# Experts of 256 slots: one matmul of 512 columns for both parts of the tokens, and down products with the weights streaming

## Chip, cores and metric

One core of one Trainium2 chip. The metric is device microseconds of one execution; smaller is better. TensorE is written PE, VectorE DVE, ScalarE ACT, GpSimd POOL, SyncE SP.

## The reference, cut to what matters

Two layers of a token-mixing block followed by a channel-mixing block; 1024 tokens of 1024 float32 numbers each. The channel mixing of the second layer is what the change touches: a router gives every token two of eight experts, and an expert is a gated two-layer network with 2816 inner features.

```python
logits = jnp.dot(xt, w_router).astype(jnp.float32)
top_logits, top_idx = lax.top_k(logits, TOP_K)
top_w = jax.nn.softmax(top_logits, axis=-1)
...
h = jax.nn.silu(lax.ragged_dot(xs, w_gate, group_sizes)) * lax.ragged_dot(xs, w_up, group_sizes)
ys = lax.ragged_dot(h, w_down, group_sizes) * top_w.reshape(-1)[order][:, None]
out = jax.ops.segment_sum(ys, tok, num_segments=n_tok)
...
x = _layernorm(DEEPNORM_ALPHA * x + (1.0 + g2) * ff, ln2_g[layer], ln2_b[layer])
```

## The kernel before, in words

**Precision.** Products of float32 are made from two parts of each operand: `split` (L350) rounds a tile to the format fp32r on ACT (the high part) and takes the rest on DVE (the low part); `wsplit` (L361) does it for weights. `mm3` (L354) then accumulates three matmuls in PSUM: high x high, high x low and low x high. In `mm3(out, a, b)` the first operand of each matmul is the one that is loaded into PE (stationary), and the second streams through it, one column after the other.

**Experts.** The eight experts are sorted by their number of tokens, and expert r (r = 0 to 7) has a fixed number of slots, `CAPS[r]` = 328, 280, 272, 264, 260, 256, 256, 256 (L36); what goes beyond is left to `overflow`. `moe` (L1342) runs the experts in a row:

- `gather` (L1094) fetches the tokens' rows from memory with indirect DMAs of POOL. `expert_in` (L1116) transposes them on PE (tile `xt`, L1125), scales them on ACT and splits them: tiles `xs`, features in partitions, slots in columns, high and low parts in tiles of their own.
- `expert_up` (L1147): for each of 22 blocks of 128 inner features, the gate and the up weights (1024 x 128 each, tiles `ew`) are split, and for each of the two and each of 8 slices k of the 1024 inputs `mm3` runs with the weights stationary and the slots streaming (tiles `eg` and `eu`, N columns each). ACT takes the Silu of `eg` from PSUM (L1166), DVE multiplies it by `eu` from PSUM (L1167), and the result is split into the tiles `eh`. Weights arrive by two DMAs of 1 MB from SP's queue for each two blocks (L1140).
- `expert_down` (L1172): for each quarter `dp` of the 1024 outputs, two blocks j of 128 outputs are accumulated over the 22 inner blocks, again with the weights stationary (tiles `dw`) and the N slots streaming (tile `ed`, outputs in partitions). ACT scales by the gate column `gcol` (L1194), PE transposes the result back to one row per slot (tile `yp`, L1200), and ACT copies it to `yr` (L1202), which a DMA of POOL writes to `ys`. For the last expert, `last_expert` (L1306) adds it to the tokens' rows instead (L1332), normalizes them (`finish`, L1278) and writes them to the output.

While expert 7's up products run, hooks (L1368) combine the results of the other experts for all 1024 tokens, in eight tiles: `combine` (L1285) gathers two result rows per token by indirect DMA, adds them on DVE (L1299), normalizes on DVE and ACT and applies two rows of the layer norm on POOL (`gain`, L782). While expert 1's run, hooks prepare the residual.

`gate_row` (L324) makes a row of the conditioning gate, one plus the gate, the same in all partitions: per 128 columns DVE makes a diagonal matrix and PE multiplies it by ones in float32.

**Order and buffers.** The order of each engine's instructions is set when the program is built, by a scheduler that simulates a timeline (L1465); engines work through their instructions in that order and wait on semaphores. PSUM has six banks for products (`bank`, L115) and two for transposes (`tbank`, L121). Six tiles `ws` hold three pairs of high and low weight parts (L75), four tiles hold raw weights (L91), three `tmp` tiles hold intermediate results (L76), and 32 tiles of 4 KB per partition (`s4`, L88) hold the rest.

Of the kernel before, what the change touches and what calls it, by code (L numbers as in the profile page):

```python
# [6 lines left out]
F32 = mybir.dt.float32  # L7
F32R = mybir.dt.float32r
I32 = mybir.dt.int32
U32 = mybir.dt.uint32  # L10
AF = mybir.ActivationFunctionType
# [22 lines left out]


CAPS = (328, 280, 272, 264, 260, 256, 256, 256)  # L36
PITCH = 1280
OVB = sum(CAPS[:-1])
FAR = 1 << 16
# [27 lines left out]
class Trunk:  # L67
# [1048 lines left out]
    def expert_in(self, r, rows, AB):  # L1116
        nc = self.nc
        N = CAPS[r]
        A, B = AB
        xs = [[self.s4([P, 3, N], F32R, f"xs{r}{x}{i}") for i in range(3)] for x in "hl"]  # L1120
        for k in range(KT):
            ps = self.tbank(f"xt{r}{k}")
            for c, t in enumerate(rows):
                n = min(P, N - c * P)
                nc.tensor.transpose(ps[:, c * P:c * P + n], t[:n, k * P:(k + 1) * P], self.ident[:n, :n])  # L1125
            u = self.tmp([P, N], f"xu{r}{k}")
            nc.scalar.activation(u, ps[:, :N], AF.Identity, bias=B[:, k:k + 1], scale=A[:, k:k + 1])  # L1127
            self.split(xs[0][k // 3][:, k % 3], xs[1][k // 3][:, k % 3], u)
        return xs

    def expert_w(self, r, f, n, queue=None):

# [14 lines left out]
    def expert_up(self, r, xs, ahead, hook):  # L1147

        nc = self.nc
        N = CAPS[r]  # L1150
        hs = [[self.s4([P, 3, N], F32R, f"eh{r}{x}{i}") for i in range(8)] for x in "hl"]
        for fb in range(0, NF, 2):
            if ahead and fb < 4:
                ws = lambda j: ahead[fb // 2 + 1](j) if fb else ahead[j](0)
            else:
                ws = self.expert_w(r, fb, 2)
            for f in (fb, fb + 1):
                pss = []
                for i, (hi, lo) in enumerate(ws(f - fb)):
                    ps = self.bank(f"e{'gu'[i]}{r}{f}")  # L1160
                    for k in range(KT):
                        self.mm3(ps[:, :N], (hi[:, k], lo[:, k]), [xs[x][k // 3][:, k % 3] for x in range(2)],
                                 k == 0, k == KT - 1)
                    pss.append(ps)
                sg = self.tmp([P, N], f"es{r}{f}")
                nc.scalar.activation(sg, pss[0][:, :N], AF.Silu)  # L1166
                nc.vector.tensor_tensor(sg, sg, pss[1][:, :N], op=OP.mult)  # L1167
                self.split(hs[0][f // 3][:, f % 3], hs[1][f // 3][:, f % 3], sg)
            hook(fb // 2)
        return hs  # L1170

    def expert_down(self, r, hs, gcol, ys, last=None):  # L1172
        nc, w = self.nc, self.w
        N, e = CAPS[r], self.ereg[r]
        nch = (N + P - 1) // P
        wv = w["moe_w_down"][0][bass.ds(e, 1)].rearrange("e (f p) n -> p (e f) n", p=P)
        if last is None:
            yr = [self.s4([P, D], F32, f"yr{r}{c}") for c in range(nch)]
        for dp in range(4):
            pss = [self.bank(f"ed{r}{dp}{j}") for j in range(2)]  # L1180
            for f0 in range(0, NF, 8):
# [14 lines left out]
            for c in range(nch):  # L1196
                n = min(P, N - c * P)
                ps = self.tbank(f"yp{r}{dp}{c}")
                for j in range(2):
                    nc.tensor.transpose(ps[:n, j * P:(j + 1) * P], yt[j][:, c * P:c * P + n], self.ident)  # L1200
                if last is None:
                    nc.scalar.activation(yr[c][:n, dp * 256:(dp + 1) * 256], ps[:n, :256], AF.Copy)  # L1202
                else:
                    last(c, dp, ps)
        if last is not None:
            return
        for c in range(nch):
            n = min(P, N - c * P)
            nc.gpsimd.dma_start(ys[BASE[r] + c * P:BASE[r] + c * P + n, :], yr[c][:n])  # L1209
# [96 lines left out]
    def last_expert(self, acc, rows, out):  # L1306
# [19 lines left out]

        done = []

        def f(c, dp, ps):
            n = min(P, N - c * P)  # L1330
            x, sl = xs[c], slice(dp * 256, (dp + 1) * 256)
            nc.vector.scalar_tensor_tensor(x[:n, sl], ps[:n, :256], ws[c][:n], x[:n, sl], op0=OP.mult, op1=OP.add)  # L1332
            if dp == 3:
                self.finish(x[:n], [a[:n] for a in rows], f"l{c}")
                s = nc.gpsimd.indirect_dma_start(out=out, out_offset=at(c, n, raw), in_=x[:n], in_offset=None,
                                                 bounds_check=S - 1, oob_is_err=False)
                for o in done:
                    self.tc.declare_no_dep(s.ins, o.ins, reason="each slot belongs to one token")
                done.append(s)
        return f  # L1340

    def moe(self, l, xn, AB, pieces, back, out):  # L1342
# [16 lines left out]
        hook = none = lambda i: None  # L1359
        for r in range(NE):  # L1360
            last = None
            if r == 1:
                res = self.residual(xn, xr)
                hook = lambda i: res(i) if i < NT else None
            elif r == NE - 1:
                rows = self.rows(l, 2, 1.0, pool=self.s4)
                comb = self.combine(ys, xr, acc, rows, out)
                hook = lambda i: comb(i - i // 4) if i % 4 < 3 and i < 10 else None  # L1368
# [4 lines left out]
                xs = self.expert_in(r + 1, self.gather(r + 1, xn), AB)  # L1373
            else:
                last = self.last_expert(acc, rows, out)
            self.expert_down(r, hs, gcol, ys, last)


def build(tc, out, **w):
# [89 lines left out]
```

## Time and profile before

| | |
|---|---|
| median of three runs | 3360.11 us (3357.93 to 3360.26) |
| the profiled execution | 3357.9 us |
| its span | 3356.2 us |
| mean granted TensorE clock | 0.985 |
| PE busy | 97% of the span |
| DVE, ACT, POOL busy | 55%, 36%, 12% |
| memory traffic | 496 MB, 148 GB/s on the mean |

The profile is one execution. The span runs from its first to its last instruction; the execution's own time is 1.7 us longer. Busy times of matmuls overlap one another, since a matmul begins before the one ahead of it has left the array, so a busy PE says that it always has work, and the distance between starts says what a matmul costs. A group of instructions is named by engine, line, and tiles out<-in; a line can be that of a helper (`split` and `mm3` above all), so the tiles tell the place.

### The profile page before, as it was taken

Reading aid. Unit: us, or ns where it says so; the run is one execution under the profiler, and the core shown is the slowest. Engines: PE = TensorE matmul, PEld = TensorE weight load, DVE = VectorE, ACT = ScalarE, POOL = GpSimd, SP = SyncE. Lnnn points to the kernel's source line nnn. Section 1 sums busy time; section 2 is a strip of 40 time slices with the busy share of each in tenths; the row PEclk is TensorE's granted clock in tenths of the full one; section 3 lists DMA queues with packets and bytes.
Section 4 is the critical chain, followed back from the end, with each engine's and each line's share of the span. In section 5 each row is a group of like instructions: output and inputs, shape, how many; then the busy total and the mean of one; then the engine's idle time right before and its main releaser. Section 6 shows DMA issues by size and latency. Waiting matters only on the chain. (4 is left out here: it accounts for less than half of the span.)

```text
span 3356.2 us, 50542 instructions
## 1 busy us (share of the span) xinstructions
PE 3263.0 (97%) x20832; PEld 2989.2 (89%) x20832; DVE 1829.7 (55%) x2699; ACT 1197.5 (36%) x1787; POOL 400.9 (12%) x291
## 2 busy tenths in 40 slices
PE   8999989999999999999799999999999999999998
PEld 7878768888888889888689999999999999999998
DVE  6888984343333262455444375454554545455685
ACT  4322222111111243222143444444454454545453
POOL 2000021001000114101100041000000000000152
PEclk8999999999999999999899999999999999999999
DMA  8545543111111133121155476555656665565784
GB/s 249 160 147 160 190 150 131 51 38 51 51 51 51 44 120 102 57 87 55 51 184 160 144 244 218 175 179 170 194 180 194 198 192 176 190 200 193 258 299 164
DMA packets 439901, 495.59 MB, mean 148 GB/s; under 512 B 20265, under 2 KB 405549, under 8 KB 439664
## 3 DMA queue, kind: packets, MB, share of 16 engines
q1 hardware_dynamic: 425528, 445.25, 41.7%
q0 software_dynamic: 13840, 46.95, 4.0%
q8 instruction: 165, 2.70, 0.4%
q14 instruction: 72, 0.59, 0.1%
q10 hardware_dynamic: 296, 0.10, 0.0%
HBM read 447.84 MB, written 44.63 MB: 147 GB/s over the span
## 5 line engine op out<-in xcount | busy, mean ns | idle before, releaser
L854 DVE TENSOR_TENSOR xres<-xres,fd 128x512 f32<-128x512 f32 x160 | 109.1, 687 | 92.9 <-PE fd L359 91.7
L830 DVE TENSOR_TENSOR fsg<-fsg,fu 128x512 f32<-128x512 f32 x44 | 30.3, 688 | 232.6 <-PE fu L359 232.6
L1167 DVE TENSOR_TENSOR es<-es,eu 128x256 f32<-128x256 f32 (+5 forms) x176 | 76.6, 435 | 121.3 <-PE eu L359 120.2
L306 DVE SCALAR_TENSOR_TENSOR acc<-ag,cond,acc 128x256 f32<-128x256 f32 x240 | 108.8, 495 | 34.8 <-DMA ag<-in_ada_w_dram 34.8
L839 POOL TENSOR_TENSOR fd<-fd,G 128x1024 f32<-128x1024 f32 x22 | 52.6, 2410 | 590.4 <-DMA fd<-in_ffn_w_down_dram 444.0
L1110 POOL DMA_INDIRECT xg<-xn,ixc x21 | 24.8, 1182 | 541.2 <-DVE es L1167 193.0
L1209 POOL DMA_DIRECT2D ys<-yr x19 | 10.9, 574 | 621.6 <-ACT yr L1202 621.6
L351 ACT ACTIVATE hh<-fsg 128x512 fp32r<-128x512 f32 x44 | 27.8, 632 | 120.6 <-DVE fsg L830 120.6
L1166 ACT ACTIVATE es<-eg 128x256 f32<-128x256 f32 (+5 forms) x176 | 66.8, 380 | 2.2 <-PE eg L359 2.1
L829 ACT ACTIVATE fsg<-fg 128x512 f32<-128x512 f32 x44 | 25.9, 588 | 86.6 <-PE fg L359 83.9
L359 PE MATMUL L0mix<-L0woh,L0yl 128*128 128x512 f32 x128 | 50.3, 401 | 4.5 <-DVE L0yl L352 4.5
L357 PE MATMUL L0mix<-L0woh,L0yh 128*128 128x512 f32 x128 | 50.9, 398 | 2.8 <-ACT L0yh L351 2.8
L1125 PE MATMUL xt<-cst,xg 128*128 128x128 f32 (+2 forms) x168 | 32.1, 277 | 20.8 <-DMA xg<-xn,ixc 20.1
L358 PE MATMUL L0mix<-L0wol,L0yh 128*128 128x512 f32 x128 | 51.0, 398 | 1.0 <-DVE L0wol L352 1.0
L357 PE MATMUL L1mix<-L1woh,L1yh 128*128 128x512 f32 x128 | 51.9, 405 | 0.0
L358 PE MATMUL L1mix<-L1wol,L1yh 128*128 128x512 f32 x128 | 51.4, 402 | 0.0
L359 PE MATMUL L1mix<-L1woh,L1yl 128*128 128x512 f32 x128 | 51.1, 399 | 0.0
L1125 PEld LDWEIGHTS xt<-cst,xg 128*128 128x128 f32 (+2 forms) x168 | 22.4, 146 | 27.0 <-ACT ew001h L351 18.0
L1127 ACT ACTIVATE xu<-xt,B,A 128x256 f32<-128x256 f32 (+5 forms) x64 | 35.3, 575 | 25.5 <-PE xt L1125 22.8
L681 DVE RECIPROCAL L1rs<-L1rs 128x512 f32<-128x512 f32 x8 | 26.8, 3353 | 24.8 <-ACT L1rs L680 24.8
L352 DVE TENSOR_TENSOR hl<-fsg,hh 128x512 fp32r<-128x512 f32 x44 | 30.5, 693 | 15.0 <-ACT hh L351 15.0
L359 PEld LDWEIGHTS L0mix<-L0woh,L0yl 128*128 128x128 f32 x128 | 24.4, 190 | 10.4 <-DVE L0yl L352 5.6
(5658 smaller groups left out, 12950.1 us busy)
## 6 DMA issues: line engine op xcount, KB each, us to landing
er<-in_moe_w_gate_dram SPq DMA_DIRECT2D x86, 1024.0 KB, 5.4
er<-in_moe_w_up_dram SPq DMA_DIRECT2D x86, 1024.0 KB, 5.7
dr<-in_moe_w_down_dram SPq DMA_DIRECT2D x64, 1024.0 KB, 5.4
ag<-in_ada_w_dram SPq DMA_DIRECT2D x160, 256.0 KB, 2.9
dr<-in_moe_w_down_dram SPq DMA_DIRECT2D x32, 768.0 KB, 4.6
fg<-in_ffn_w_gate_dram SPq DMA_DIRECT2D x11, 1024.0 KB, 5.9
fu<-in_ffn_w_up_dram SPq DMA_DIRECT2D x11, 1024.0 KB, 5.6
fd<-in_ffn_w_down_dram SPq DMA_DIRECT2D x11, 1024.0 KB, 4.9
```

The costliest lines, as they stand in the source:

```text
L306: V.scalar_tensor_tensor(acc, raw[:, kk], c, acc, op0=OP.mult, op1=OP.add)
L352: (eng or self.nc.vector).tensor_tensor(lo, src, hi.bitcast(F32), op=OP.subtract)
L357: mm(out, a[0], b[0], start=start, stop=False)
L358: mm(out, a[0], b[1], start=False, stop=False)
L359: mm(out, a[1], b[0], start=False, stop=stop)
L830: nc.vector.tensor_tensor(sg, sg, pss[1], op=OP.mult)
L839: nc.gpsimd.tensor_tensor(draw[:, j], draw[:, j], G, op=OP.mult)
L854: nc.vector.tensor_tensor(xs, xs, ps, op=OP.add)
L1125: nc.tensor.transpose(ps[:, c * P:c * P + n], t[:n, k * P:(k + 1) * P], self.ident[:n, :n])
L1127: nc.scalar.activation(u, ps[:, :N], AF.Identity, bias=B[:, k:k + 1], scale=A[:, k:k + 1])
L1166: nc.scalar.activation(sg, pss[0][:, :N], AF.Silu)
L1167: nc.vector.tensor_tensor(sg, sg, pss[1][:, :N], op=OP.mult)
```

## The change

For experts whose slots number 256 (r = 5, 6, 7; `HALF`):

- `expert_in` puts the high and the low part of a slice of the tokens side by side in one tile, 512 columns.
- `expert_up` streams both parts under the high weights in one matmul of 512 columns, and the high part under the low weights in one of 256 columns that adds to the first half. The two halves of the PSUM bank are then added: ACT copies the second half to a tile `eb`, DVE adds the first. Silu and product read that tile.
- `expert_down_rows` replaces `expert_down`: the hidden tiles `eh` are stationary (128 slots at a time) and the weights stream, 512 outputs at a time, so that the results come out with one row per slot and need no transpose back. DVE multiplies them from PSUM by a gate row (`grow`), which is made once, ahead of expert 4's up products. `last_expert` takes 512 columns at a time from that.

```diff
@@ -34,6 +34,7 @@
 
 
 CAPS = (328, 280, 272, 264, 260, 256, 256, 256)
+HALF = 256
 PITCH = 1280
 OVB = sum(CAPS[:-1])
 FAR = 1 << 16
@@ -1117,7 +1118,12 @@
         nc = self.nc
         N = CAPS[r]
         A, B = AB
-        xs = [[self.s4([P, 3, N], F32R, f"xs{r}{x}{i}") for i in range(3)] for x in "hl"]
+        if N == HALF:
+            pair = [self.s4([P, 2, 2, N], F32R, f"xs{r}{i}") for i in range(4)]
+            dst = lambda k: (pair[k // 2][:, k % 2, 0], pair[k // 2][:, k % 2, 1])
+        else:
+            xs = [[self.s4([P, 3, N], F32R, f"xs{r}{x}{i}") for i in range(3)] for x in "hl"]
+            dst = lambda k: (xs[0][k // 3][:, k % 3], xs[1][k // 3][:, k % 3])
         for k in range(KT):
             ps = self.tbank(f"xt{r}{k}")
             for c, t in enumerate(rows):
@@ -1125,8 +1131,8 @@
                 nc.tensor.transpose(ps[:, c * P:c * P + n], t[:n, k * P:(k + 1) * P], self.ident[:n, :n])
             u = self.tmp([P, N], f"xu{r}{k}")
             nc.scalar.activation(u, ps[:, :N], AF.Identity, bias=B[:, k:k + 1], scale=A[:, k:k + 1])
-            self.split(xs[0][k // 3][:, k % 3], xs[1][k // 3][:, k % 3], u)
-        return xs
+            self.split(*dst(k), u)
+        return pair if N == HALF else xs
 
     def expert_w(self, r, f, n, queue=None):
 
@@ -1159,9 +1165,24 @@
                 for i, (hi, lo) in enumerate(ws(f - fb)):
                     ps = self.bank(f"e{'gu'[i]}{r}{f}")
                     for k in range(KT):
-                        self.mm3(ps[:, :N], (hi[:, k], lo[:, k]), [xs[x][k // 3][:, k % 3] for x in range(2)],
-                                 k == 0, k == KT - 1)
+                        if N == HALF:
+                            uk = xs[k // 2][:, k % 2]
+                            two = uk.rearrange("p x n -> p (x n)")
+                            if k == 0:
+                                nc.tensor.matmul(ps, hi[:, k], two, start=True, stop=False)
+                            nc.tensor.matmul(ps[:, :N], lo[:, k], uk[:, 0], start=False, stop=False)
+                            if k:
+                                nc.tensor.matmul(ps, hi[:, k], two, start=False, stop=k == KT - 1)
+                        else:
+                            self.mm3(ps[:, :N], (hi[:, k], lo[:, k]), [xs[x][k // 3][:, k % 3] for x in range(2)],
+                                     k == 0, k == KT - 1)
                     pss.append(ps)
+                if N == HALF:
+                    both = self.tmp([P, 2, N], f"eb{r}{f}")
+                    for i in range(2):
+                        nc.scalar.activation(both[:, i], pss[i][:, N:], AF.Copy)
+                        nc.vector.tensor_tensor(both[:, i], both[:, i], pss[i][:, :N], op=OP.add)
+                        pss[i] = both[:, i]
                 sg = self.tmp([P, N], f"es{r}{f}")
                 nc.scalar.activation(sg, pss[0][:, :N], AF.Silu)
                 nc.vector.tensor_tensor(sg, sg, pss[1][:, :N], op=OP.mult)
@@ -1169,13 +1190,44 @@
             hook(fb // 2)
         return hs
 
-    def expert_down(self, r, hs, gcol, ys, last=None):
+    def expert_down_rows(self, r, hs, grow, ys, last=None):
+
+        nc, w = self.nc, self.w
+        e = self.ereg[r]
+        wv = w["moe_w_down"][0][bass.ds(e, 1)].rearrange("e (f p) n -> p (e f) n", p=P)
+        if last is None:
+            yr = [self.s4([P, D], F32, f"yr{r}{c}") for c in range(2)]
+        for dh in range(2):
+            sl = slice(dh * 512, (dh + 1) * 512)
+            pss = [self.bank(f"ed{r}{dh}{c}") for c in range(2)]
+            for f0 in range(0, NF, 4):
+                fn = min(4, NF - f0)
+                raw = self.raw([P, fn, 512], f"dr{r}{dh}{f0}")
+                nc.sync.dma_start(raw, wv[:, f0:f0 + fn, sl])
+                for g in range(0, fn, 2):
+                    hi, lo = self.wsplit(raw[:, g:g + 2], f"dw{r}{dh}{f0 + g}")
+                    for j in range(2):
+                        f = f0 + g + j
+                        for c in range(2):
+                            hk = [hs[x][f // 3][:, f % 3, c * P:(c + 1) * P] for x in range(2)]
+                            self.mm3(pss[c], hk, (hi[:, j], lo[:, j]), f == 0, f == NF - 1)
+            for c in range(2):
+                if last is None:
+                    nc.vector.tensor_tensor(yr[c][:, sl], pss[c], grow[:, sl], op=OP.mult)
+                else:
+                    y = self.tmp([P, 512], f"yt{r}{dh}{c}")
+                    nc.vector.tensor_tensor(y, pss[c], grow[:, sl], op=OP.mult)
+                    last(c, sl, y)
+        if last is None:
+            for c in range(2):
+                nc.gpsimd.dma_start(ys[BASE[r] + c * P:BASE[r] + (c + 1) * P, :], yr[c])
+
+    def expert_down(self, r, hs, gcol, ys):
         nc, w = self.nc, self.w
         N, e = CAPS[r], self.ereg[r]
         nch = (N + P - 1) // P
         wv = w["moe_w_down"][0][bass.ds(e, 1)].rearrange("e (f p) n -> p (e f) n", p=P)
-        if last is None:
-            yr = [self.s4([P, D], F32, f"yr{r}{c}") for c in range(nch)]
+        yr = [self.s4([P, D], F32, f"yr{r}{c}") for c in range(nch)]
         for dp in range(4):
             pss = [self.bank(f"ed{r}{dp}{j}") for j in range(2)]
             for f0 in range(0, NF, 8):
@@ -1198,12 +1250,7 @@
                 ps = self.tbank(f"yp{r}{dp}{c}")
                 for j in range(2):
                     nc.tensor.transpose(ps[:n, j * P:(j + 1) * P], yt[j][:, c * P:c * P + n], self.ident)
-                if last is None:
-                    nc.scalar.activation(yr[c][:n, dp * 256:(dp + 1) * 256], ps[:n, :256], AF.Copy)
-                else:
-                    last(c, dp, ps)
-        if last is not None:
-            return
+                nc.scalar.activation(yr[c][:n, dp * 256:(dp + 1) * 256], ps[:n, :256], AF.Copy)
         for c in range(nch):
             n = min(P, N - c * P)
             nc.gpsimd.dma_start(ys[BASE[r] + c * P:BASE[r] + c * P + n, :], yr[c][:n])
@@ -1326,11 +1373,10 @@
 
         done = []
 
-        def f(c, dp, ps):
-            n = min(P, N - c * P)
-            x, sl = xs[c], slice(dp * 256, (dp + 1) * 256)
-            nc.vector.scalar_tensor_tensor(x[:n, sl], ps[:n, :256], ws[c][:n], x[:n, sl], op0=OP.mult, op1=OP.add)
-            if dp == 3:
+        def f(c, sl, y):
+            n, x = P, xs[c]
+            nc.vector.scalar_tensor_tensor(x[:, sl], y, ws[c], x[:, sl], op0=OP.mult, op1=OP.add)
+            if sl.stop == D:
                 self.finish(x[:n], [a[:n] for a in rows], f"l{c}")
                 s = nc.gpsimd.indirect_dma_start(out=out, out_offset=at(c, n, raw), in_=x[:n], in_offset=None,
                                                  bounds_check=S - 1, oob_is_err=False)
@@ -1359,6 +1405,8 @@
         hook = none = lambda i: None
         for r in range(NE):
             last = None
+            if r + 1 < NE and CAPS[r + 1] == HALF < CAPS[r]:
+                grow = self.gate_row(l, 5, self.s4)
             if r == 1:
                 res = self.residual(xn, xr)
                 hook = lambda i: res(i) if i < NT else None
@@ -1373,7 +1421,10 @@
                 xs = self.expert_in(r + 1, self.gather(r + 1, xn), AB)
             else:
                 last = self.last_expert(acc, rows, out)
-            self.expert_down(r, hs, gcol, ys, last)
+            if CAPS[r] == HALF:
+                self.expert_down_rows(r, hs, grow, ys, last)
+            else:
+                self.expert_down(r, hs, gcol, ys)
 
 
 def build(tc, out, **w):
```

## Rows read from the trace of the kernel before

**Rows 1.** The page of the profile: its first line

```profile
span 3356.2 us, 50542 instructions
```

**Rows 2.** Windows: up and down stages of experts 5, 6 and 7, in order

```profile
core 0: us, PE busy (x) PEld busy (x) DVE busy (x) ACT busy (x) POOL busy (x), PEclk, DMA share, GB/s
2746.30:2873.60 127.30, 127.30 (x1064) 127.25 (x1063) 70.29 (x88) 60.30 (x91) 3.92 (x5) 1.00 0.61 197
2873.60:2940.00 66.40, 66.40 (x559) 66.40 (x558) 30.70 (x34) 34.71 (x54) 0.00 (x0) 1.00 0.57 179
2940.00:3068.80 128.80, 127.38 (x1063) 127.18 (x1062) 70.28 (x92) 59.98 (x90) 6.29 (x6) 1.00 0.61 195
3068.80:3135.10 66.30, 66.30 (x558) 66.30 (x557) 30.64 (x34) 34.71 (x54) 0.00 (x0) 1.00 0.60 195
3135.10:3276.20 141.10, 132.98 (x1062) 131.63 (x1061) 119.16 (x136) 80.16 (x111) 66.21 (x43) 0.96 0.86 300
3276.20:3341.00 64.80, 64.80 (x544) 64.80 (x542) 38.07 (x40) 26.20 (x32) 15.85 (x9) 1.00 0.55 177
```

**Rows 3.** Waits of PE (engine, line <- whom: us, times, longest), 2550 to 3356

```profile
PE eg L359 <- DVE ew7180l L352: 3.9, 1, 3.9
...
PE eu L359 <- DVE ew6191l L352: 1.4, 1, 1.4
```

**Rows 4.** Timeline of PE (start, us, instruction): 256 columns, first and last of 18

```profile
2900.96 0.28 PE L357 MATMUL ed<-eh5h,dw5181h 128*128 128x256 f32 x1
...
2903.00 0.28 PE L359 MATMUL ed<-eh5h,dw5181l 128*128 128x256 f32 x1
```

**Rows 5.** Timeline of PE: 512 columns, dense layer's down products, first and last of 28

```profile
606.31 0.39 PE L357 MATMUL fd<-fdw2h,hh 128*128 128x512 f32 x1
...
612.43 0.39 PE L357 MATMUL fd<-fdw3h,hh 128*128 128x512 f32 x1
```

**Rows 6.** Timeline of PE in the mixer: from 512 to 256 columns

```profile
84.72 0.39 PE L359 MATMUL L0cb<-u0h,L0cbw0l 128*128 128x512 f32 x1
84.95 0.28 PE L357 MATMUL L0v<-L0vw00h,u0h 128*128 128x256 f32 x1
85.06 0.28 PE L358 MATMUL L0v<-L0vw00l,u0h 128*128 128x256 f32 x1
```

**Rows 7.** Timeline of PE: a pair of transposes among down products, expert 5

```profile
2900.62 0.38 PE L1200 MATMUL yp<-cst,yt 128*128 128x128 f32 x2
2900.76 0.36 PE L359 MATMUL ed<-eh5h,dw5181l 128*128 128x256 f32 x1
```

**Rows 8.** The gate rows' tile: its matmuls (min/median/max ns, first and last start)

```profile
L334 PE MATMUL gr<-dg,cst x48: 270/275/377, 324.6 to 1508.9; 128*128 128x128 f32 x48
```

**Rows 9.** Groups of DVE and ACT in expert 5's up stage (busy us, mean ns)

```profile
L1167 DVE TENSOR_TENSOR es<-es,eu 128x256 f32<-128x256 f32 x21 | 8.9, 422 | 14.4 <-PE eu L359 14.4
...
L352 DVE TENSOR_TENSOR eh5l<-es,eh5h 128x256 fp32r<-128x256 f32 x21 | 8.8, 419 | 0.0
...
L1166 ACT ACTIVATE es<-eg 128x256 f32<-128x256 f32 x22 | 8.1, 366 | 0.0
```

**Rows 10.** The same groups of DVE in expert 7's up stage

```profile
L352 DVE TENSOR_TENSOR eh7l<-es,eh7h 128x256 fp32r<-128x256 f32 x21 | 10.9, 519 | 0.0
...
L1167 DVE TENSOR_TENSOR es<-es,eu 128x256 f32<-128x256 f32 x21 | 8.6, 408 | 2.8 <-PE eu L359 2.4 <-ACT es L1166 0.5
```

**Rows 11.** The page's groups: a DVE operation of 128x512 with a PSUM operand

```profile
L854 DVE TENSOR_TENSOR xres<-xres,fd 128x512 f32<-128x512 f32 x160 | 109.1, 687 | 92.9 <-PE fd L359 91.7
```

**Rows 12.** Timeline: a weight split ends on DVE, PE's first use of it

```profile
2805.75 1.23 DVE L352 TENSOR_TENSOR ew5110l<-er,ew5110h 128x1024 fp32r<-128x1024 f32 x1 [0.54 <-ACT ew5110h L351]
...
2810.28 0.28 PE L357 MATMUL eg<-xs5h,ew5110h 128*128 128x256 f32 x1
```

**Rows 13.** Timeline: PE's last matmul, DVE's last operations on results

```profile
3340.76 0.28 PE L359 MATMUL ed<-eh7h,dw73161l 128*128 128x256 f32 x1
...
3341.98 0.88 DVE L1332 SCALAR_TENSOR_TENSOR lx<-yp,lc,lx 128x256 f32<-128x256 f32 x2 [6.38 <-PE yp L1200]
```

## The prediction

> **What bounds the kernel now.** I read the windows of the stages first, then the waits of TensorE (PE), then the distances between matmul starts, then VectorE (DVE) and ScalarE (ACT) in the same stages. The span is 3356.2 us [rows 1]. The change touches experts 5, 6 and 7, which have 256 slots each; each has an "up" stage (gate and up products) and a "down" stage. [...] Expert 7's up stage differs: 141.1 us instead of 127.3, clock 0.96, DVE busy 119.2 us, DMA 0.86 and GpSimd (POOL) 66.2 us [rows 2], because the combination of the other experts' results runs beside it. There PE waits for weight splits of DVE, 3.9 us in one case [rows 3].
>
> The busy times of matmuls overlap, so I price a matmul by the distance between starts. With 256 columns: 17 steps from 2900.96 to 2903.00, 120.0 ns [rows 4]. With 512: 27 steps from 606.31 to 612.43, 226.7 ns [rows 5]. Two matmuls of 256 take 240.0, so one of 512 saves 13.3 ns: a matmul has a fixed cost of about 13 ns beside its columns.
>
> **Up stages.** Per operand, block of 128 features and k, three matmuls of 256 (360.0 ns) become one of 512 and one of 256 (346.7 ns). There are 22 x 2 x 8 = 352 such steps in an expert: 352 x 13.3 ns = 4.7 us. That sizes may alternate freely is not shown over a run of them; where the mixer goes from 512 to 256, the starts lie 0.23 and then 0.11 us apart [rows 6], so a change of size costs nothing there. Bounds: nothing gained (0), or the fixed cost of the 256-wide matmul vanishing too in the shadow of the wide one, 352 x 26.6 ns = 9.4 us; I take 4.7, which the transition shows. An alternation that loses is not excluded: a pair of float32 transposes put among the matmuls costs 0.22 us [rows 7], but that is another kind of operation.
>
> Added per block: two ACT copies from PSUM (366 ns each, by the Silu of the same shape) and two DVE adds with one PSUM operand (422 ns, by the product of the same shape) [rows 9]. That is 44 x 0.366 = 16 us of ACT and 44 x 0.422 = 18.6 us of DVE per expert. In experts 5 and 6 they lie beside PE: DVE comes to 70.3 + 18.6 = 89 of about 122 us, ACT to 76. The queues are in order, so a copy that waits for PE holds the weight splits behind it. What covers this: a split that ends on DVE at 2806.98 is first needed by PE at 2810.28 [rows 12], 3.3 us of lead, against about 0.4 to 0.8 us of added work between two splits. I cost it at nothing; were the lead gone, each block would lose what it lacks, and there are 66.
>
> In expert 7's up stage there is no such cover. DVE has 119.2 us of work there and gets 18.6 more. The Silu product moves besides: it read PSUM and now reads two SBUF tiles. In this stage an operation of two SBUF inputs has gone from 419 to 519 ns, while the product with a PSUM input has not grown (422 and 408) [rows 9, 10]; 22 x 0.1 = 2.2 us more. DVE then has 140.0 us of work. [...] Bounds for the stage: 136.4 us (PE's gain of 4.7 kept, and splits as late as now) and 161.9 (140.0 plus all of the 21.9 us that DVE idles now). The added work fills idle time first, and I leave 5 us idle for the start of the stage, before results are gathered: 145 us, 3.9 more than now.
>
> **Down stages.** Each has 4 x 2 x 22 x 3 = 528 matmuls of 256: 63.4 us; it gets 2 x 22 x 2 x 3 = 264 of 512: 59.8 us. Gain 3.5 us per expert, 10.5 in all. That is the order of operands of the dense layer, whose rows gave 226.7 ns [rows 5]. The 16 transposes of each result go: in the trace they come in pairs; a pair and one matmul fill the time from 2900.62 to 2900.96, so a pair takes 0.22 us [rows 4, 7]; 24 pairs are 5.3 us. The weight traffic is the same, 12 DMAs per expert on SP's queue, now in rows of 2 KB instead of 1; 1 MB is used up in 24 x 0.2267 = 5.4 us instead of 5.8, and the DMA share of 0.57 to 0.60 [rows 2] leaves room. Splits go from 24 to 22 with the same elements. ACT loses its scaled copies and the copies of the transposed results; DVE gets 4 products of 128x512 per expert, 0.69 us each [rows 11], beside PE. Costed at nothing; PE covers it.
>
> **Gate row.** Once, ahead of expert 4's up stage: 8 float32 matmuls of 128 columns. Earlier gate rows show 48 records for three rows, two per matmul, 275 ns each [rows 8]. As pairs of transposes cost 0.22 us [rows 7], 8 pairs are 1.8 us of PE; bounds 0 (in a gap) and 8 x 2 x 0.275 = 4.4. Its 8 + 2 DVE operations lie beside PE.
>
> **The end.** PE's last matmul starts at 3340.76, is over 0.28 later, and DVE is through with the last results at 3341.98 + 0.88 = 3342.86 [rows 13], 1.8 us behind PE. [...]
>
> **The sum.** -4.7 (up 5) -4.7 (up 6) +3.9 (up 7) -10.5 (down) -5.3 (transposes) +1.8 (gate row) +0.6 (end) = -18.9 us. The profiled execution took 3357.9 us (its span and 1.7 around it), so 3339.0. The median of the runs shown is 2.2 above it; against that, 3341.
>
> [...]
>
> **The rivals.**
> *Nothing is late in expert 7.* DVE's long operations there are stretched ones, and the order of instructions is planned anew, so the combination could slip into the down stage, where DVE is busy 38.1 of 64.8 us [rows 2]. Then the stage is at 122 to 136 us: 8.6 to 23 us better than I take, 3318 to 3332. Against it: DVE would have to do 140 us of work in that time. Chance 0.15.
> *The longer chain holds the splits (slower).* Copy, add, Silu, product, rounding, rest go back and forth between ACT and DVE, both in order, and the splits stand behind them. If a block lacks t us, 66 blocks lose 66 t; from t = 0.29 on the gain of 18.9 is gone. With t = 0.6, the time is 3341 + 40 = 3381. For it: in expert 7 it would set in first. Against it: the lead of 3.3 us [rows 12], and DVE at 73%. Chance 0.13.
> *The fixed cost is not saved.* The 13.3 ns could belong to the weight load or the columns in a way that alternation and the new order of operands bring back. Then the 4.7 + 4.7 + 10.5 us go, the rest of the sum stays, +1.0, and the time is 3361. Against it: both widths show the same 13.3 [rows 4, 5] and the transition shows nothing extra [rows 6]. Chance 0.07. [...]
> *The change does not do what it says:* the planner puts the gate row or the longer splits so that PE waits at the borders, a few us each: 3345 to 3355. Chance 0.05.
>
> **How the numbers follow.** My forecast has the remaining 0.60. Its own range, from the bounds of expert 7's stage and of the gate row, is 3332 to 3358. The best case below it reaches to 3318; I let the range begin at 3328 and end at 3358, which leaves out most of the slower rival, part of the third and a part of the first. About 0.2% (6.7 us) is what a measurement can tell from no change: faster takes the forecast but for its worst end (0.57), the first rival (0.15) and most of the last (0.05): 0.77. Same: 0.10, from the third rival and the forecast's end. Slower: 0.13, the second rival.
>
> **What would show it.** In the changed profile: starts 0.23 and 0.12 us apart in turn in the up stages; up stages of experts 5 and 6 at about 122 to 124 us with no wait of PE, down stages at 61 to 62; no yp transposes there; DVE near 89 us in an up stage; expert 7's up stage longer than 141 us with DVE busy about 140 and PE's waits on splits grown. I am wrong if the steps of 512 and 256 take over 0.36 us, if PE waits in experts 5 and 6, or if expert 7's up stage gets shorter.

## The result and the profile after

The changed kernel takes 3338.44 us (median of four runs, 3337.98 to 3340.30), the kernel before 3359.65 us in the same comparison: ratio 0.9939, 95% interval 0.9926 to 0.9951, so 21 us or 0.6% faster. A second comparison (run e12 below) gave 3338.5 and 0.9943 [0.9926, 0.9959]. The forecast was 3341, with 3328 to 3358 as its range and faster as the likeliest case.

First the page of the changed kernel, lines 1 and 2: PE has 1880 instructions fewer, DVE 144 more.

```profile
span 3338.6 us, 46978 instructions
...
PE 3241.7 (97%) x18952; PEld 2884.3 (86%) x18952; DVE 1889.3 (57%) x2843; ACT 1221.3 (37%) x1873; POOL 403.1 (12%) x291
```

The windows of the six stages, to be laid beside [rows 2] (a stage runs from its first matmul to the first of the next; columns as there):

```profile
2751.90:2875.60 123.70, 123.70 (x712) 107.74 (x711) 84.25 (x131) 72.47 (x133) 3.80 (x5) 1.00 0.63 205
2875.60:2937.50 61.90, 61.90 (x282) 51.12 (x282) 32.88 (x37) 30.48 (x42) 0.00 (x0) 1.00 0.57 187
2937.50:3061.20 123.70, 123.27 (x705) 107.14 (x704) 84.98 (x136) 71.24 (x130) 5.84 (x6) 1.00 0.64 204
3061.20:3123.10 61.90, 61.90 (x282) 51.10 (x281) 32.78 (x37) 30.46 (x42) 0.00 (x0) 1.00 0.63 204
3123.10:3260.00 136.90, 126.64 (x690) 106.95 (x689) 129.32 (x168) 86.36 (x142) 67.81 (x43) 0.98 0.86 295
3260.00:3323.10 63.10, 62.84 (x280) 51.54 (x278) 47.35 (x50) 28.92 (x34) 16.80 (x9) 1.00 0.59 211
```

In order, the stages have lost 3.6, 4.5, 5.1, 4.4, 4.2 and 1.7 us, 23.5 in all. Expert 4's up stage, into which the gate row was put, grew from 126.25 to 128.06 us (by the starts of its first matmul and of the down stage's), 1.8. What lies behind the end of the last matmul grew by 0.2. The span of this one execution is 17.6 us shorter and not 21.5, because its expert 4 began 3.8 us later; PE's order up to there is unaltered, and that start lies between 2550.1 and 2557.2 us over all the profiles here: scatter of what comes earlier.

The waits of PE, to be laid beside [rows 3]: experts 5 and 6 have one of 0.4 us, expert 7 has the others.

```profile
PE eu L1173 <- DVE ew7111l L353: 3.5, 1, 3.5
PE eg L1173 <- DVE ew7210l L353: 2.3, 1, 2.3
PE eu L1172 <- ACT ew7181h L352: 1.3, 1, 1.3
PE eu L1172 <- ACT ew7211h L352: 0.9, 1, 0.9
PE eu L1173 <- DVE ew761l L353: 0.9, 1, 0.9
PE eu L1173 <- DVE ew6191l L353: 0.4, 1, 0.4
...
```

The granted clock of TensorE in expert 7's up stage is 0.98 on the mean. With two of these waits (3.5 and 2.3 us) it fell to 0.51 and 0.53, the means of two stretches of 3.4 us; the first of them:

```profile
3194.20:3197.60 3.40, 3.40 (x12) 2.91 (x11) 3.40 (x3) 1.10 (x2) 3.16 (x2) 0.51 0.97 278
```

The timeline of PE in expert 5's up stage: after 512 columns the next start comes 0.23 us later, after 256 columns 0.11 to 0.12.

```profile
2800.97 0.39 PE L1175 MATMUL eu<-xs,ew581h 128*128 128x512 f32 x1
2801.20 0.27 PE L1173 MATMUL eu<-xs,ew581l 128*128 128x256 f32 x1
2801.32 0.40 PE L1175 MATMUL eu<-xs,ew581h 128*128 128x512 f32 x1
2801.55 0.28 PE L1173 MATMUL eu<-xs,ew581l 128*128 128x256 f32 x1
```

The groups of DVE in expert 7's up stage, to be laid beside [rows 10]:

```profile
L353 DVE TENSOR_TENSOR eh7l<-es,eh7h 128x256 fp32r<-128x256 f32 x19 | 18.1, 953 | 0.0
L1188 DVE TENSOR_TENSOR es<-es,eb 128x256 f32<-128x256 f32 x20 | 11.2, 560 | 0.6 <-ACT es L1187 0.3
...
L1184 DVE TENSOR_TENSOR eb<-eb,eg 128x256 f32<-128x256 f32 x20 | 8.2, 409 | 0.0
L1184 DVE TENSOR_TENSOR eb<-eb,eu 128x256 f32<-128x256 f32 x20 | 8.1, 406 | 0.0
```

The added adds, with one operand in PSUM, take what they were priced at. The product, which now reads two SBUF tiles, went from 408 to 560 ns, and the rest `eh7l` from 519 to 953. DVE is busy 94% of this stage.

### The profile page after: what moved, and what is told of

Read it like the earlier page. It is cut to its first block, busy times and chain, and to the rows that moved or that the text cites. A ratio compares the mean times of both kernels' runs of the same rounds, so it can differ in the third digit from the quotient of the medians.

```text
span 3338.6 us, 46978 instructions
## 1 busy us (share of the span) xinstructions
PE 3241.7 (97%) x18952; PEld 2884.3 (86%) x18952; DVE 1889.3 (57%) x2843; ACT 1221.3 (37%) x1873; POOL 403.1 (12%) x291
## 5 line engine op out<-in xcount | busy, mean ns | idle before, releaser
L1188 DVE TENSOR_TENSOR es<-es,eu 128x328 f32<-128x328 f32 (+4 forms) x110 | 49.0, 446 | 86.2 <-PE eu L360 85.4
L1187 ACT ACTIVATE es<-eg 128x328 f32<-128x328 f32 (+4 forms) x110 | 42.5, 387 | 0.0
```

## The experiments

"Expert 7" is the length of its up and down stages together: 205.9 us before, 200.0 after. The ratios are against the kernel before.

**e1: the up products alone.** The kernel before with the new `expert_in` and `expert_up`; one place of it, seen from the changed kernel:

```diff
-            if CAPS[r] == HALF:
-                self.expert_down_rows(r, hs, grow, ys, last)
-            else:
-                self.expert_down(r, hs, gcol, ys)
+            self.expert_down(r, hs, gcol, ys, last)
...
```

> Only the up stages are changed; down products, transposes back and the end are as before. Theory (PE sets the length of experts 5 and 6, DVE's late splits set that of expert 7): up stages 5 and 6 at about 124 us, expert 7's up at 135 to 139, down stages as before (66.4, 66.3, 64.8); in all 11 to 13 us faster than before, about 3347. Rival (expert 7's up stage only got shorter because of the changed down stages around it): expert 7's up stays at 141 or grows to 145, in all 4 to 8 us faster.

Measured: 3360.89 us (median of ten), ratio 1.0004 [0.9994, 1.0014]: nothing gained. Windows of expert 7's two stages:

```profile
3129.50:3268.80 139.30, 126.56 (x695) 107.39 (x694) 123.50 (x164) 87.19 (x143) 62.11 (x41) 0.98 0.85 294
3268.80:3343.50 74.70, 70.31 (x558) 69.38 (x556) 51.38 (x56) 32.49 (x44) 20.12 (x12) 0.95 0.51 170
```

Up stages 5 and 6 got 3.6 and 4.6 us shorter as expected. Expert 7 took 214.0 us, 8.1 more than before, and gave it all back: PE is idle there for 17.1 us (length less PE's busy time) instead of 8.1. The time was missed by 14 us by the theory, and it lies beyond the rival's too: what DVE owes in the up stage appears in the down stage, 74.7 instead of 64.8 us, as a part of the last up products comes after the first of the down products there.

**e2: the down products alone.** The changed kernel with the old `expert_in` and `expert_up`:

```diff
...
-                                nc.tensor.matmul(ps, hi[:, k], two, start=False, stop=k == KT - 1)
...
+                        self.mm3(ps[:, :N], (hi[:, k], lo[:, k]), [xs[x][k // 3][:, k % 3] for x in range(2)],
+                                 k == 0, k == KT - 1)
...
```

> Only the down products are changed, up stages run three matmuls of 256 as before. Theory: down stages 5 and 6 at 61.9 us instead of 66.4, expert 7's at 61 to 63, gate row 1.8 us, expert 7's up stage as before at 141; in all 8 to 11 us faster than before, about 3350. Rival (expert 7's up stage profits from the down change): expert 7's up at 137 or less, in all 12 to 15 us faster.

Measured: 3342.82 us, 0.9955 [0.9938, 0.9972], 17 us (9 to 21 by the interval). Down stages 61.8, 61.8 and 59.9 us. The rival holds, though the median gain is larger than its 12 to 15 us: expert 7's up stage, with the very products of before, takes 136.5 instead of 141.1 us.

```profile
3130.00:3266.50 136.50, 129.32 (x1058) 127.32 (x1057) 122.61 (x136) 79.15 (x108) 67.93 (x43) 1.00 0.91 315
3266.50:3326.40 59.90, 59.90 (x266) 49.35 (x264) 41.20 (x37) 23.12 (x23) 17.51 (x9) 1.00 0.51 178
```

Expert 7 is at 196.4 us, 9.5 less than before, where its own matmuls and transposes explain 5.2 (3.5 + 1.3, and 0.4 for the pairs of expert 6 that ran in its up stage). Most of the other 4.3 us is the granted clock. In the kernel before, the granted clock was 0.50 for 10.2 us of this stage, in two stretches that came with PE's waits of 2.4 and 3.9 us:

```profile
3177.20:3180.60 3.40, 3.40 (x19) 3.40 (x17) 3.40 (x4) 1.38 (x3) 0.55 (x1) 0.50 0.78 239
3248.90:3255.70 6.80, 5.98 (x28) 5.98 (x29) 4.82 (x8) 1.45 (x2) 3.59 (x2) 0.50 0.42 152
```

Their 47 matmuls start 0.21 us apart and not 0.12, which makes about 4 us (an estimate). In e2 the longest wait of PE in this stage is 1.7 us, and the clock stays at 1.00. So PE's busy time in the up stage falls from 132.98 to 129.32 us for the very same products (0.4 of it for the pairs), and its idle time only from 8.1 to 7.2. A difference that can be seen in the order of events: expert 6's rows are handed to the DMA 0.5 us after expert 7's first matmul, not 5.1 us as before (there the last results went through ACT, PE and ACT again), and the first combining add on DVE comes 15.8 us into expert 7, not 21.7.

**e3: no copies and adds.**

```diff
-                if N == HALF:
-                    both = self.tmp([P, 2, N], f"eb{r}{f}")
-                    for i in range(2):
-                        nc.scalar.activation(both[:, i], pss[i][:, N:], AF.Copy)
-                        nc.vector.tensor_tensor(both[:, i], both[:, i], pss[i][:, :N], op=OP.add)
-                        pss[i] = both[:, i]
```

> Leaves out the two copies of ACT and the two adds of DVE per block: Silu and product read only the first halves of the PSUM banks, so the products of the high weights with the tokens' low parts are missing from the result; PE's work is the same. Theory (cover by PE in experts 5 and 6, DVE the limit in expert 7): up stages 5 and 6 stay at 123.7 us within 0.3, expert 7's up falls from 136.9 to 130 to 134; against the changed kernel 3 to 7 us faster. Rival (the added work lies in idle time in expert 7 as well, and its waits come from the combination alone): expert 7's up stays at 136 to 138, in all no difference.

Measured: 3330.04 us, 0.9915 [0.9899, 0.9932]. Up stages 5 and 6 at 123.7 and 124.0 us, expert 7's two stages at 133.1 and 60.7:

```profile
3118.30:3251.40 133.10, 126.69 (x705) 108.16 (x704) 118.94 (x137) 79.37 (x109) 66.94 (x44) 0.99 0.92 322
3251.40:3312.10 60.70, 60.32 (x265) 49.30 (x263) 40.95 (x37) 23.10 (x23) 14.02 (x9) 1.00 0.51 179
```

The theory holds: the copies and adds cost nothing in experts 5 and 6 and 6.2 us in expert 7 (200.0 to 193.8): PE's idle time there goes from 10.5 to 6.8 us, and the stretches at a granted clock of about 0.5 from 6.8 to 3.4 us.

**e4: high weights first.**

```diff
+                    if N == HALF:
+                        for k in range(KT - 1):
+                            nc.tensor.matmul(ps, hi[:, k], xs[k // 2][:, k % 2].rearrange("p x n -> p (x n)"),
+                                             start=k == 0, stop=False)
+                        for k in range(KT):
+                            nc.tensor.matmul(ps[:, :N], lo[:, k], xs[k // 2][:, k % 2, 0], start=False, stop=False)
+                        k = KT - 1
+                        nc.tensor.matmul(ps, hi[:, k], xs[k // 2][:, k % 2].rearrange("p x n -> p (x n)"),
+                                         start=False, stop=True)
...
```

> The changed kernel with another order of the same matmuls in an up stage: seven of 512 columns under the high weights, then eight of 256 under the low weights, then the last of 512. The low parts are needed 1.6 us later. Theory (PE's waits in expert 7 are for the low parts that DVE makes late): expert 7's up falls from 136.9 to 131 to 134; experts 5 and 6 at 122.5 to 123.7 us (122.5 if each change between 512 and 256 columns costs something, 123.7 if not); 4 to 8 us faster than the changed kernel. Rival (DVE's throughput is the limit, so that a later deadline only moves the waits): expert 7's up stays at 135 to 138, within 2 us of the changed kernel.

Measured: 3340.57 us, 0.9942 [0.9925, 0.9958]; expert 7 at 205.1, up stages 5 and 6 at 123.6 and 122.9. A miss: the later deadline did not shorten expert 7, it grew by 5 in this profile (of the slowest of the four runs), and the waits of PE are again for DVE and also for ACT. Its up stage, 143.4 us, lies beyond the rival's 135 to 138 too; in the total the rival's "within 2 us" about came out (2.1). Expert 5's up stage is 0.1 us shorter than in the changed kernel, expert 6's 0.9, of which 0.6 are a wait that the changed kernel has there and this run has not (0.4 in the list of waits, 0.6 by the starts). So the changes of size cost little. The matmuls of one product in expert 5's up stage:

```profile
2799.66 1.77 PE L1169 MATMUL eu<-xs,ew581h 128*128 128x512 f32 x7
2801.27 1.11 PE L1172 MATMUL eu<-xs,ew581l 128*128 128x256 f32 x8
2802.22 0.40 PE L1174 MATMUL eu<-xs,ew581h 128*128 128x512 f32 x1
```

Seven of 512 columns in a row take 1.61 us, 0.230 each, where the dense layer's took 0.2267 [rows 5]; eight of 256 take 0.95, 0.119 each.

**e5: three of 256 again for expert 7 alone.**

```diff
-        if N == HALF:
+        if N == HALF and r < NE - 1:
...
```

> The changed kernel, but expert 7's up stage runs three matmuls of 256 again, without the copies and adds; experts 5 and 6 and all down stages as changed. Theory (in expert 7 the copies and adds on a full DVE cost more than PE gains): expert 7's up and down together 196 us, as with the down change alone (136.4 + 59.9), instead of 200.0; up stages 5 and 6 at 123.7; 3 to 4 us faster than the changed kernel, about 3335. Rival (those 3.6 us between two profiles are scatter, and the wide matmul gains PE time in expert 7 too): expert 7 at 200 or more, no faster or 2 to 4 us slower than the changed kernel.

Measured: 3332.68 us, 0.9918 [0.9901, 0.9934], below the changed kernel in all four of its runs. Expert 7: 196.9 us, as in e2, and again at a clock of 1.00.

```profile
3118.10:3255.00 136.90, 129.22 (x1057) 127.22 (x1056) 122.40 (x136) 79.27 (x108) 67.87 (x43) 1.00 0.90 315
3255.00:3315.00 60.00, 60.00 (x266) 49.41 (x264) 41.22 (x37) 23.13 (x23) 17.51 (x9) 1.00 0.50 175
```

The theory holds: in expert 7 the wide matmul, with its copies and adds, costs more than it brings (200.0 us against 196.9).

**e6: expert 6's rows written later.**

```diff
+                if r == NE - 2:
+                    for _ in range(2):
+                        nc.scalar.activation(yr[c], yr[c], AF.Copy)
```

> The changed kernel with four added ACT copies of expert 6's result rows onto themselves (1.06 us each) ahead of their writing, so that the rows that expert 7's combination gathers are written about 2 to 5 us later. Theory (with the down change the combination starts 15.5 us after expert 7's begin instead of 21.7, and the DVE work of expert 7 is spread over that much more time): the first combining add comes 3 to 6 us later, and expert 7's up and down together grow by 2 to 6 us from 200.0. Rival (expert 7's up stage got shorter because its order was planned anew): it stays within 1 us of 200.0.

Measured: one run of 3336.16 us; expert 7 at 202.3. The first combining add came 23.3 us after expert 7's first matmul, 7.8 later than in the changed kernel:

```profile
3140.02 1.28 DVE L1349 SCALAR_TENSOR_TENSOR cx<-cy,tw,cx 128x1024 f32<-128x1024 f32 x1 [3.45 <-DMA cy<-ys,rslot]
```

The growth of 2.3 us against one profile of the changed kernel, and of 1.0 against the other (e12), is too small beside their scatter to settle anything. PE is idle 12.0 us here and its granted clock about 0.5 for 10.2 us; the two profiles of the changed kernel have 10.5 and 9.8 us, and 6.8 and 13.6. Inconclusive.

**e7: copies and adds made twice.**

```diff
                         nc.scalar.activation(both[:, i], pss[i][:, N:], AF.Copy)
                         nc.vector.tensor_tensor(both[:, i], both[:, i], pss[i][:, :N], op=OP.add)
+                        nc.scalar.activation(both[:, i], pss[i][:, N:], AF.Copy)
+                        nc.vector.tensor_tensor(both[:, i], both[:, i], pss[i][:, :N], op=OP.add)
                         pss[i] = both[:, i]
```

> The changed kernel with each copy of ACT and each add of DVE made twice per block, in all three experts: 18 us more of DVE and 16 us more of ACT per up stage. Theory (covered by PE in experts 5 and 6, not in 7): up stages 5 and 6 stay at 123.7 within 0.5 us with DVE at about 102 us; expert 7's up and down grow by 8 to 18 us from 200.0. Rival (the chain between ACT and DVE is what just holds the splits): up stages 5 and 6 grow by 3 us or more each.

Measured: 3352.54 us in one run. Windows of the up stages 5, 6 and 7 (DVE is the third pair of numbers):

```profile
2750.50:2874.30 123.80, 123.80 (x713) 107.77 (x712) 95.92 (x171) 83.59 (x175) 3.78 (x5) 1.00 0.63 205
2936.10:3059.80 123.70, 123.30 (x705) 107.13 (x704) 96.33 (x176) 82.74 (x170) 5.75 (x6) 1.00 0.63 204
3121.70:3271.70 150.00, 132.32 (x706) 111.56 (x705) 141.95 (x212) 100.72 (x184) 63.07 (x43) 0.95 0.82 280
```

The theory holds: where PE covers, twice the work is free (123.7 and 123.8 us by the starts), and in expert 7, now at 213.7 us, it costs 13.7. The added work is smaller than expected: DVE's busy time in the up stages of experts 5 and 6 grew by 11 to 12 us and ACT's by 11 to 12, not by 18 and 16. In part this is because they were priced by the duration of one operation: in the trace adds that follow one another take 0.41 us each but start 0.33 us apart. The forecast's slower rival, a chain that holds the splits, is out for experts 5 and 6.

**e8: no layer-norm rows on POOL.**

```diff
             self.normalize(x, f"m{t}")
-            self.gain(x, rows)
```

> Leaves out the two POOL operations of the layer norm's rows in the combination of expert 7's stage, so the rows of the combined tokens lack weight and bias of the last norm. Theory (the stretched DVE operations of two SBUF inputs are those that run beside POOL's): in expert 7's up stage the rests eh7l fall from 953 ns to 420 to 460, the Silu products from 560 to 420 to 440, weight splits of over 2 us vanish; expert 7's up and down together fall from 200.0 to 186 to 194. Rival (the stretching comes from the DMA traffic or the memory): the durations stay over 500 ns, expert 7 within 2 us of 200.0.

Measured: 3317.73 us in one run. Groups of DVE in expert 7's up stage, then the windows of its two stages:

```profile
L1188 DVE TENSOR_TENSOR es<-es,eb 128x256 f32<-128x256 f32 x20 | 8.3, 414 | 0.4 <-ACT es L1187 0.2
...
L353 DVE TENSOR_TENSOR eh7l<-es,eh7h 128x256 fp32r<-128x256 f32 x19 | 7.9, 418 | 0.0
```

```profile
3116.00:3240.20 124.20, 124.03 (x705) 107.13 (x704) 108.79 (x172) 87.18 (x144) 30.46 (x31) 1.00 0.95 331
3240.20:3300.10 59.90, 59.90 (x265) 49.36 (x263) 37.73 (x46) 27.50 (x32) 4.27 (x5) 1.00 0.58 209
```

The rests went from 953 to 418 ns, the products from 560 to 414, and PE has no gap left: 124.2 us, the length of experts 5 and 6, with all copies and adds in it and more DMA traffic per microsecond than before (331 GB/s). Expert 7 is at 184.2 us, below the range of the theory. So DVE was full (busy 129.32 us of this stage in the changed kernel, 108.79 here) because POOL's operations stretched its own. In the kernel before the longest wait of PE [rows 3] is of this kind; timelines of DVE and of POOL:

```profile
3243.35 6.31 DVE L352 TENSOR_TENSOR ew7180l<-er,ew7180h 128x1024 fp32r<-128x1024 f32 x1
...
3243.90 2.39 POOL L789 TENSOR_TENSOR cx<-cx,ln_b 128x1024 f32<-128x1024 f32 x1
3246.24 2.33 POOL L789 TENSOR_TENSOR cx<-cx,ln_g 128x1024 f32<-128x1024 f32 x1
```

A weight split that takes 1.21 us elsewhere in this stage took 6.31, about its own time and that of the two POOL operations beside it (5.93). By these records the split began 0.55 us before the first of the two and ended 1.09 us after the second. How POOL's operations stretch those of DVE is not shown.

**e9: six of eight wide matmuls as two of 256.**

```diff
-                            if k:
-                                nc.tensor.matmul(ps, hi[:, k], two, start=False, stop=k == KT - 1)
+                            if 0 < k < KT - 1:
+                                for x in range(2):
+                                    nc.tensor.matmul(ps[:, x * N:(x + 1) * N], hi[:, k], uk[:, x], start=False, stop=False)
+                            elif k:
+                                nc.tensor.matmul(ps, hi[:, k], two, start=False, stop=True)
```

> The changed kernel with six of the eight matmuls of 512 columns of every up product made as two of 256 into the two halves of the bank; all else, the copies and adds too, as changed. Theory (13 ns of fixed cost per matmul): 44 x 6 x 13.3 ns = 3.5 us more per up stage, so up stages 5 and 6 at 127.2 instead of 123.7. [...] Rival (the weight load of each matmul sets the distance): 128 or more.

Measured: 3340.57 us in one run; up stages 5 and 6 at 125.9 and 125.7 us. Timeline of PE, four steps apart:

```profile
2796.31 0.28 PE L1173 MATMUL eu<-xs,ew581l 128*128 128x256 f32 x1
...
2797.74 0.28 PE L1173 MATMUL eu<-xs,ew581l 128*128 128x256 f32 x1
```

A step of three takes (2797.74 - 2796.31) / 4 = 0.358 us. The stages grew by 2.1 us over 264 steps, 8 ns for each matmul. That is less than the theory's 13.3 ns, mostly since the matmul of 512 columns itself is dearer here than in [rows 5] (0.230 against 0.2267 us, e4). The rival's 128 us did not come.

**e10 and e11: the norm of the combination without POOL**, in the changed kernel (e10) and in e5's form (e11):

```diff
-            self.normalize(x, f"m{t}")
-            self.gain(x, rows)
+            self.finish(x, rows, f"m{t}")
```

> The changed kernel, with the combination's norm made by two DVE operations per tile of tokens, as the last expert's rows have it, instead of one of DVE and two of POOL; the same result. Theory (POOL's two operations hold back those of DVE with two SBUF inputs): 8 x 1.5 us more of DVE work, but none of the stretched operations; expert 7's up and down together 185 to 192 us instead of 200.0, 8 to 15 us faster than the changed kernel. Rival (what counts is DVE's own work): expert 7 at 198 or more.

> As the run before, and expert 7's up stage with three matmuls of 256 again, without copies and adds. Theory (without the stretched operations DVE has room for copies and adds, so that the wide matmul pays in expert 7 too): expert 7's up and down at 187 to 191 us, 1 to 4 us slower than the wide form with the same norm. Rival (DVE is still full): 2 to 4 us faster than the wide form with the same norm, as it was with POOL's operations.

Measured: e10 3327.06 us, 0.9901 [0.9883, 0.9918]; e11 3325.65 us, 0.9896 [0.9880, 0.9913]. Both beat the changed kernel, by 11 and 13 us. Windows of expert 7's up stage, e10 and then e11:

```profile
3121.40:3250.00 128.60, 124.63 (x705) 107.03 (x705) 117.12 (x174) 86.44 (x140) 27.35 (x30) 1.00 0.92 319
```

```profile
3123.00:3251.40 128.40, 127.63 (x1057) 126.91 (x1057) 109.84 (x144) 76.58 (x106) 30.77 (x32) 1.00 0.95 330
```

Expert 7 is at 188.7 and 188.4 us, in both at a clock of 1.00. The theory of e10 holds. For e11 neither expectation came out: the two forms are equal here. In e10 PE is idle 4.0 us in the up stage, in e11 0.8; the difference is about what the wide matmul would have gained.

**e12: the changed kernel again.**

> The changed kernel once more, unaltered, for the scatter of the stages that the other runs are compared with. Theory: up stages 5 and 6 within 0.2 us of 123.7, down stages within 0.2 of 61.8, expert 7's up and down within 2.5 us of 200.0, in all 3336 to 3341. Rival (expert 7's length varies from execution to execution by as much as the runs differ): 203 or more, or 197 or less.

Measured: 3338.5 us; up stages 123.7 and 123.9, down stages 61.8 and 61.9, expert 7 at 137.7 + 63.7 = 201.4, all as expected. So expert 7 scatters by 1.4 us between these two profiles, with 6.8 and 13.6 us at a granted clock of about 0.5, and e2 and e5 (196.4 and 196.9) lie outside of that.

## Why the prediction was right, and which term of it was not

The direction, the sum (-18.9 forecast, -21.2 by the medians) and the mechanism of experts 5 and 6 were right. Expert 7's up stage was not: it got shorter, which the prediction itself had named as a sign of being wrong. That the sum came so close is in part luck, as errors of both signs fell together.

- **Up stages 5 and 6** (forecast -4.7 each, the transposes apart): before the change PE was busy for 127.30 of 127.30 and 127.38 of 128.80 us of them, at a granted clock of 1.00 [rows 2], so but for 1.4 us the stages were as long as PE's work. They lost 3.6 us in expert 5, and 3.6 in expert 6 between e2 (127.36) and the changed kernel (123.76). The step saved 10 ns instead of 13.3. The prediction's doubt, that sizes may not alternate freely, accounts for the smaller part: without the alternation (e4) the stages are 0.1 to 0.2 us shorter, waits taken off. The larger part is the price of the wide matmul, taken from another layer: in the up stages 512 columns start 0.230 us apart even in a row (e4) and not 0.2267 [rows 5]. Why is not shown. The cover held as costed (e3, e7), with DVE at 84 to 85 us and not 89.
- **Down stages** (-10.5, and -5.3 for transposes): 4.5 and 4.4 us for experts 5 and 6, where the rows give 4.8 for the matmuls and the six of eight pairs that ran in the stage itself; 4.9 for expert 7 with the down change alone (64.8 to 59.9). In the changed kernel expert 7's down stage lost only 1.7 us, as the last up products run 3.2 us into it.
- **Gate row and end**: 1.8 and 0.2 us, forecast 1.8 and 0.6. No run shows the forecast's 0.6 us for the end: after the change DVE's last product starts 0.04 us behind the modelled end of PE's last matmul.
- **Expert 7's up stage** (forecast +3.9, to 145 us) was the step that failed: measured -4.2, to 136.9. The working took the 141.1 us of the kernel before as the ground on which DVE's added work comes to lie. It left out that the down change acts on this stage by itself: 136.5 us (e2). It also gave the low clock of this stage (0.96 in [rows 2]) no term: 10.2 us at a granted clock of 0.50, which cost about 4 us by the estimate under e2, stood in that ground, and they are gone in e2, where PE's waits are shorter. Against the ground of e2 the copies and adds cost about what was forecast, with part of it in the next stage: 200.0 or 201.4 us for expert 7 against 196.4, 3.6 to 5.0 us lost where the columns alone would have gained 3.6. In the first of these two profiles that is 3.3 us more of idle PE, and 6.8 us at a granted clock of about 0.5 where e2 has none. For the stretching of operations with two SBUF inputs (419 to 519 ns, [rows 9, 10]) the working added 2.2 us, to the Silu product alone; this product grew by 0.15 us each, and the rests `eh7l`, which were not thought of, from 519 to 953 ns.
- **The range.** Its own bounds, 3332 to 3358, are those of expert 7's stage alone; with the gate row's, which the text names too, they would be 3331 to 3361.
- **The rivals.** "Nothing is late in expert 7" did not happen: PE idles 10.3 us there. "The longer chain holds the splits" is shown wrong for experts 5 and 6. "The fixed cost is not saved" is wrong for the down stages and mostly wrong for the up stages: [rows 4, 5] give 13.3 ns as the one difference between the two widths, and a matmul saved in an up stage was worth 8 to 10. Waits at the borders did not come: expert 4 grew by the gate row's 1.8 us alone.
- **What stays open** is why the waits of PE in expert 7 are shorter in e2, at the longest 1.7 us instead of 3.9, and why the clock does not fall there. The earlier start of the combination is seen, but e6, which put it back, lies within the scatter. That the planned order of DVE's instructions differs around it was not separated from it.

In sum, of the 21 us the down products bring 17 (e2, 9 to 21 by its interval), alone; the up products bring nothing alone (e1) and, by the medians, 4 on top of the down products. The intervals of e2 and of the change overlap, so this 4 rests on the stages: 7.2 gained in experts 5 and 6 and about 4 lost in expert 7.

## What to carry to other kernels

Count matmuls as well as columns: at the same columns each matmul saved was worth 8 to 13 ns here, and with the operands exchanged the results came out in the layout wanted, without transposes. Price added elementwise work stage by stage: the same copies and adds were free where PE covered them (DVE at 68 to 69%) and cost 6 us where DVE was near full (94%). When an engine is full, look first at what stretches its instructions, and take a stage's ground from the kernel with the other parts of the change already in it. Read the granted clock of a stage before its length is used: in expert 7 some 4 us of 141 (the estimate under e2) went in 10.2 us at a granted clock of 0.50.

## What the runs showed that I had not expected

POOL's 16 elementwise operations of the combination cost expert 7 16 us (200.0 to 184.2 without them); DVE operations of 1.2 us took up to 6.3 us beside them in the kernel before (3.9 us of PE's wait, [rows 3]), and moving the work to DVE itself made the kernel 11 us faster (e10), though DVE then does two operations of 1.28 us in place of one of 0.81 (e8) eight times, some 14 us more. And matmuls of 256 columns are no cheaper than those of 260: before the change they start 120.0 ns apart [rows 4], those of expert 4 with 260 columns 118.9 ns on the mean of some 500 steps.
